# The prompt's mixer input in two tiles, loaded by chunks, and a place of its own for every second mixer weight

## The chip, the cores and the metric

One core of one Trainium2 chip. The time is device microseconds of one execution of the whole program; the number that is compared is the median of several runs. Engines: TensorE (PE: matmuls; its weight loads are called PEld), VectorE (DVE), ScalarE (ACT), GpSimd (POOL) and SyncE (SP, which here only issues transfers). ACT issues transfers as well: all the weight loads stand in its queue.

## The reference

An encoder layer, applied to two groups of tokens with the same weights: the "prompt" (1024 tokens, `s = 0`) and the "sample" (512 tokens, `s = 1`), each with 16 meta tokens put in front. Model width 1024, feed-forward width 2816, all in fp32:

```python
mix = jnp.concatenate([oa, ob], axis=-1)        # the two attention groups' outputs
h   = x + mix @ w_out                            # the "mixer"
n   = rms_norm(h, g_ffn)
gate = conv3(n @ w_ff_gate)                      # depthwise, width 3, over positions
h   = h + (gelu(gate) * (n @ w_ff_up)) @ w_ff_down
y   = rms_norm(h, g_final)
```

Before it come an RMS norm, one projection `w_in`, and two kinds of attention. The change touches only `mix @ w_out` of the prompt.

## The kernel before

Matrices lie transposed: features on the 128 partitions, tokens along the row. A width of 1024 is eight blocks `k` (or `j` on the output side) of 128. Each fp32 product is made of three matmuls in a rounded format (fp32r): the operand is split into `hi` (a cast by ACT, L125) and `lo` (the difference, by DVE or POOL, L126), and `mm3` (L129) adds `hi*hi` (L131), `hi*lo` (L132) and `lo*hi` (L133).

**Weights.** `load_weight` (L144) fetches one block of 128x1024 fp32 (512 KB) into `w_f`, a raw buffer of which there are two (`NRAW`), then writes `w_hi` and `w_lo` into the pool `g.wp`. That pool has three places for each (`NW = 3`), used in turn by all weights of the second half of the program. A cast of `w_hi` can start when the last matmul that read the place's former content is done.

**The mixer of the prompt** (`mixer_out`, L629, with `whole = False`). The 1026 columns are worked in three chunks of 344, 342 and 340. For a chunk: eight casts `xhi<-h` on ACT and eight differences `xlo<-h` on DVE (L666 to L669), then for each of the eight output blocks `j` a weight `w_out[j]`, 24 matmuls into `ps_s`, the sum with the residual (L681) and the sum of squares (L682, `add_square`, ACT and POOL). So each chunk goes through all eight weights once more, 24 weights in all. `h` is one tile, 128 x 8 x 1026; attention's output lies in `oT` in device memory and is loaded into `h` by ten transfers: seven whole blocks of 1025 columns and, for the last block, one for each chunk (L659 to L662).

**What comes before and after.** A generator interleaves the prompt's attention with the sample's mixer and conv-GLU (`merge`, L823). What is left of the sample (the last `w_down` group, L764 to L771, and its final norm, L784 to L797) is drained, and beside it the prompt's mixer begins. Then the prompt's conv-GLU runs to the end of the program; its first step (`normed`, L702) normalises chunks 0 and 1 already beside the mixer's later chunks.

**Order of the work.** On each engine the instructions stand in one fixed order, set when the program is built: a planner lays out all instructions by its own estimates of when each would be free to go, and each engine then takes its list from the top. An instruction that waits holds up all behind it on its engine. PE therefore never picks another matmul when one waits.

Of the kernel before, what the change touches and what calls it, by code (L numbers as in the profile page):

```python
# [13 lines left out]
F32 = mybir.dt.float32  # L14
F32R = mybir.dt.float32r
# [6 lines left out]
P = 128  # L22
# [118 lines left out]
                     xhi[k][:, c0:c0 + cw], xlo[k][:, c0:c0 + cw], i == 0, i == KT - 1)  # L141


def load_weight(g, src, lo_engine=None, hi_engine=None):  # L144

    nc = g.nc
    w = g.wp.tile([P, D], F32, name="w_f", tag="w_f", bufs=NRAW)
    nc.scalar.dma_start(out=w, in_=src)
    hi = g.wp.tile([P, D], F32R, name="w_hi", tag="w_hi")
    lo = g.wp.tile([P, D], F32R, name="w_lo", tag="w_lo")  # L150
    if hi_engine:
        hi_engine.tensor_copy(hi, w)
        nc.vector.tensor_tensor(out=lo, in0=w, in1=hi.bitcast(F32), op=ALU.subtract)
    else:
        split(g, hi, lo, w, lo_engine)
    return hi, lo
# [454 lines left out]
def add_square(g, tp, acc, h, j, c0, cw, eng, bufs=2):  # L611

    nc = g.nc
    hs = h[:, j, c0:c0 + cw]
    if j == 0:
        nc.scalar.activation(acc, hs, AF.Square)
    else:
        sq = tp.tile([P, cw], F32, name="sq", tag="sq", bufs=bufs)
        nc.scalar.activation(sq, hs, AF.Square)
        eng.tensor_tensor(out=acc, in0=acc, in1=sq, op=ALU.add)  # L620
# [8 lines left out]
def mixer_out(g, s, st, side, whole, tag):  # L629

    nc, tc = g.nc, g.tc
    C = SEQS[s] + 2
    h, rstd = st.h, st.rstd
    chunks = token_chunks(s)
    cm = max(w for _, w in chunks)
    with ExitStack() as es:
        mp = pool(es, g, f"fm{s}", 3, side)
        waiting = []

        def finish():  # L640
            while waiting:
                c0, cw, acc = waiting.pop(0)
                mean_rsqrt(g, mp, rstd[:, c0:c0 + cw], acc, cw, tag)

        for group in ([chunks] if whole else [[c] for c in chunks]):
            if whole:
                (xhi, xlo), base = [[x[:, k] for k in range(KT)] for x in st.x], 0
            else:
                xhi = [mp.tile([P, cm], F32R, name="xhi", tag=f"xhi{k}", bufs=2) for k in range(KT)]
                xlo = [mp.tile([P, cm], F32R, name="xlo", tag=f"xlo{k}", bufs=2) for k in range(KT)]  # L650
                base = group[0][0]
            if whole or group[0] != chunks[-1]:
                acc = mp.tile([P, sum(w for _, w in group)], F32, name="acc", tag="acc", bufs=1 if whole else 2)
            else:
                acc = st.tail.tile([P, cm], F32, name="acc_tail")[:, :group[0][1]]
            if group[0][0] == 0:

                nc.vector.memset(h[:, :, C - 1:], 0.0)
                for k in range(KT):  # L659
                    for c0, cw in [(0, C - 1)] if whole or k < KT - 1 else chunks:  # L660
                        cw = min(cw, C - 1 - c0)
                        nc.sync.dma_start(out=h[:, k, c0:c0 + cw], in_=g.oT[s][k * P:(k + 1) * P, c0:c0 + cw])  # L662
            with ExitStack() as behind:
                for mark in g.marks if whole else ():
                    behind.enter_context(tc.issue_after(mark))
                for k in range(KT):  # L666
                    for c0, cw in group:
                        b = c0 - base
                        split(g, xhi[k][:, b:b + cw], xlo[k][:, b:b + cw], h[:, k, c0:c0 + cw])  # L669
            for j in range(KT):  # L670
                w = load_weight(g, g.w_out[j])
                for c0, cw in group:
                    real = min(cw, C - 1 - c0)
                    res = mp.tile([P, cm], F32, name="res", tag="res", bufs=4)[:, :cw]
                    nc.sync.dma_start(out=res[:, :real],
                                      in_=g.xT[s][j * P:(j + 1) * P, NMETA - 1 + c0:NMETA - 1 + c0 + real])
                    if real < cw:
                        nc.vector.memset(res[:, real:], 0.0)
                    ps = g.psum.tile(P, cw, tag)
                    dense(g, ps, w, xhi, xlo, c0 - base, cw)  # L680
                    nc.vector.tensor_tensor(out=h[:, j, c0:c0 + cw], in0=ps, in1=res, op=ALU.add)  # L681
                    add_square(g, mp, acc[:, c0 - base:c0 - base + cw], h, j, c0, cw, nc.gpsimd, 1)  # L682
                    yield 24 * cw
                if j == ML:
                    finish()
            waiting += [(c0, cw, acc[:, c0 - base:c0 - base + cw]) for c0, cw in group]
        if whole:
            finish()
        else:
            st.last = waiting.pop()  # L690


def conv_glu(ctx, g, s, st, side, gb):
# [8 lines left out]
    def normed(np_, c0, cw):  # L702
        for k in range(KT):
            t = np_.tile([P, cw], F32, name="t", tag="t")
            nc.vector.scalar_tensor_tensor(out=t, in0=h[:, k, c0:c0 + cw],
                                           scalar=g.gain[:, V_GFFN + k:V_GFFN + k + 1],
                                           in1=rstd[:, c0:c0 + cw], op0=ALU.mult, op1=ALU.mult)
            split(g, xhi[k][:, c0:c0 + cw], xlo[k][:, c0:c0 + cw], t, nc.gpsimd if s == 1 or k % 2 else nc.vector)
# [13 lines left out]
    for f0 in range(0, NFF, G):  # L722
# [42 lines left out]
        def down(j, c0, cw):  # L765
            ps = g.psum.tile(P, cw, "mm")
            for i, ((ahi, alo), (dhi, dlo)) in enumerate(zip(acts, wd)):
                mm3(g, ps, dhi[:, j * P:(j + 1) * P], dlo[:, j * P:(j + 1) * P],
                    ahi[:, c0:c0 + cw], alo[:, c0:c0 + cw], i == 0, i == len(acts) - 1)
            hs = h[:, j, 1 + c0:1 + c0 + cw]  # L770
            nc.vector.tensor_tensor(out=hs, in0=ps, in1=hs, op=ALU.add)  # L771

        if grp[-1] < NFF - 1:
# [10 lines left out]
        def finish(c0, acc, sums):  # L784
            rs = rstd[:, 1 + c0:1 + c0 + cw]
            if sums:
                rsqrt_newton(g, op, rs, acc, cw)
            else:
                mean_rsqrt(g, op, rs, acc, cw)
            for k in range(KT):  # L790
                y = op.tile([P, ob, cw], F32, name="y", tag="y", bufs=2 if s == 1 else 4) if k % ob == 0 else y
                hs, gk = h[:, k, 1 + c0:1 + c0 + cw], g.gain[:, V_GFIN + k:V_GFIN + k + 1]
                if k % 4 == 3:
                    nc.scalar.activation(y[:, k % ob], hs, AF.Copy, scale=gk)
                    nc.gpsimd.tensor_tensor(out=y[:, k % ob], in0=y[:, k % ob], in1=rs, op=ALU.mult)
                else:
                    nc.vector.scalar_tensor_tensor(out=y[:, k % ob], in0=hs, scalar=gk, in1=rs,  # L797
                                                   op0=ALU.mult, op1=ALU.mult)
                if (k + 1) % ob == 0:
                    nc.sync.dma_start(out=yv[:, k + 1 - ob:k + 1, c0:c0 + cw], in_=y)  # L800

        waiting = None
        for c0 in range(0, N, cw):

            sums = s == 0 and c0 + cw == N
            acc = g.psum.tile(P, cw, "mm") if sums else op.tile([P, cw], F32, name="acc", tag="acc", bufs=ob)
            for j in range(KT):
                down(j, c0, cw)
                if sums:
                    sq = op.tile([P, cw], F32, name="sq", tag="sq_p", bufs=4 * ob)  # L810
                    nc.scalar.activation(sq, h[:, j, 1 + c0:1 + c0 + cw], AF.Square)
                    nc.tensor.matmul(acc, lhsT=g.ones_d, rhs=sq, start=j == 0, stop=j == KT - 1)
                else:
                    add_square(g, op, acc, h, j, 1 + c0, cw, nc.gpsimd if j < PADD else nc.vector, 2)
                if j == LAG and waiting:
                    finish(*waiting)
                yield 3 * len(grp) * cw
            waiting = c0, acc, sums
# [29 lines left out]
LAG = 5  # L848
PADD = 8
ML = 2  # L850
NRAW, NW = 2, 3
R1, R2 = (1.0, 1.1), (1.0, 1.0)
LEAD1, LEAD2, HOLD, STATS = -20000.0, 120000.0, 4, 26

# [2 lines left out]
def trunk_kernel(ctx, tc, g):  # L857
# [61 lines left out]
    def state(es, s, side, with_x):  # L919
        C = SEQS[s] + 2  # L920
        st = Ctx()
        hp = pool(es, g, f"fh{s}", 1, side)
        if with_x:
            st.x = [hp.tile([P, KT, C], F32R, name=nm) for nm in ("xhi", "xlo")]
        st.h = hp.tile([P, KT, C], F32, name="h")
        st.rstd = hp.tile([P, C], F32, name="rstd")
        st.tail = hp
        return st
# [105 lines left out]
```

## Time and profile before

| | |
|---|---|
| median of 3 runs | 2184.26 us (2183.82 to 2185.66) |
| profiled execution, its own time | 2184.81 us |
| span of the profile | 2182.7 us |
| PE busy | 2114.2 us, 97% of the span |
| mean granted TensorE clock | 0.989 |
| prompt's mixer, first matmul to the first `w_gate` matmul | 1309.1 to 1421.3 us |

The time of the profiled execution is 2.1 us more than its span: work ahead of the first and behind the last recorded instruction. In a row of the timeline stand the start, the duration, the engine (ACTq and SPq are the queues that issue transfers), the line, the operation with its tiles, and in square brackets how long the engine had been idle and what ended that. The durations of matmuls are modelled, and each overlaps the next: the pace is read from start to start. In a table of windows, each row gives the window, its length, each engine's busy time with the number of instructions, then the clock that was granted to PE (1.00 is full speed), the share of the transfer engines and the rate in GB/s.

### The profile page before, as it was taken

What the parts mean: (1) busy time and instruction counts of PE and PEld (TensorE: products, weight loads), DVE (VectorE), ACT (ScalarE), POOL (GpSimd) and SP (SyncE); (2) the same over time, 40 slices, a digit from 0 to 9 for tenths busy, and PEclk for the clock granted to TensorE, in tenths of its full rate; (3) what the DMA queues carried; (4) which work ended last, traced back from release to release, by engine and by line L of the source; (5) the groups of instructions that cost most, each with busy time, mean ns of one, the idle gap of its engine ahead of it and who ended that gap; (6) DMA issues with size and microseconds to landing.
All of it is one profiled execution on the core that took longest, in us unless ns stands there. A gap on an engine that the chain in (4) does not pass through costs nothing.

```text
span 2182.7 us, 32285 instructions
## 1 busy us (share of the span) xinstructions
PE 2114.2 (97%) x12442; PEld 1899.7 (87%) x12442; DVE 1319.2 (60%) x2288; ACT 1024.9 (47%) x1803; POOL 624.0 (29%) x465
## 2 busy tenths in 40 slices
PE   8999999988999999999999998999999999999997
PEld 7889999986897888898889898988888888888886
DVE  7645565777767667677777766754434344443346
ACT  6434545667756444677777645542121222112224
POOL 5763444310123222344454314530011100111004
PEclk9999999989999999999999999999999999999999
DMA  6663445563233223232332126511111111111112
GB/s 237 214 218 110 149 156 172 162 209 93 76 94 90 88 68 92 90 108 96 110 111 88 65 88 213 183 68 47 41 49 39 58 49 49 44 34 58 49 39 78
DMA packets 112137, 222.77 MB, mean 102 GB/s; under 512 B 14064, under 2 KB 65520, under 8 KB 111472
## 3 DMA queue, kind: packets, MB, share of 16 engines
q1 hardware_dynamic: 83184, 115.84, 16.7%
q10 hardware_dynamic: 28800, 104.87, 14.7%
q8 instruction: 98, 1.61, 0.3%
q14 instruction: 55, 0.45, 0.1%
HBM read 172.11 MB, written 48.55 MB: 101 GB/s over the span
## 4 chain that ended last, share of the span: by engine, by line
PE 82%; DVE 8%; ACT 3%; issue 3%; DMA 2%; POOL 1%; SPq 0%; ACTq 0%; DVEq 0%; POOLq 0%
PE ps_mm L131 20%; PE ps_mm L132 20%; PE ps_mm L133 20%; PE ps_t L467 5%; PE ps_s L446 4%; PE ps_s L447 3%; PE ps_o L482 2%; DVE p L450 1%; PE ps_o L481 1%; PE ps_o L479 1%; DVE w_lo L126 1%; PE ps_o L477 1%; PE ps_o L478 1%; DVE y L797 1%; DVE pt_lo L126 1%
## 5 line engine op out<-in xcount | busy, mean ns | idle before, releaser
L131 PE MATMUL ps_mm<-xhi,w_hi 128*128 128x512 f32 (+6 forms) x2112 | 703.4, 334 | 2.6 <-DVE hn L117 2.5
L133 PE MATMUL ps_mm<-xhi,w_lo 128*128 128x512 f32 (+6 forms) x2112 | 698.1, 331 | 0.0
L132 PE MATMUL ps_mm<-xlo,w_hi 128*128 128x512 f32 (+6 forms) x2112 | 697.9, 331 | 0.0
L131 PEld LDWEIGHTS ps_mm<-xhi,w_hi 128*128 128x128 f32 x2112 | 400.0, 190 | 28.4 <-DVE hn L117 3.1
L132 PEld LDWEIGHTS ps_mm<-xlo,w_hi 128*128 128x128 f32 x2112 | 399.4, 189 | 25.0 <-issue 0.5
L133 PEld LDWEIGHTS ps_mm<-xhi,w_lo 128*128 128x128 f32 x2112 | 399.2, 189 | 24.4 <-issue 0.5
L125 ACT CAST w_hi<-w_f 128x1024 fp32r<-128x1024 f32 x134 | 139.2, 1047 | 389.9 <-PE ps_mm L132 359.4
L126 POOL TENSOR_TENSOR a_lo<-gate,a_hi 128x512 fp32r<-128x512 f32 x66 | 100.7, 1525 | 651.8 <-ACT a_hi L125 651.6
L450 DVE TENSOR_SCALAR_CACHE_REDUCE p<-ps_s 128x1044 f32<-128x1044 f32 (+7 forms) x212 | 223.3, 1053 | 92.8 <-PE ps_s L447 77.1
L125 ACT CAST pt_hi<-ps_t 128x512 fp32r<-128x512 f32 (+8 forms) x360 | 171.0, 484 | 197.2 <-PE ps_t L467 180.3
L771 DVE TENSOR_TENSOR h<-ps_mm,h 128x512 f32<-128x512 f32 (+1 forms) x288 | 182.3, 645 | 123.7 <-PE ps_mm L133 122.8
L453 ACT ACTIVATE p<-p,nm 128x1040 f32<-128x1040 f32 (+7 forms) x212 | 215.3, 1016 | 85.2 <-DVE p L450 84.4
L126 DVE TENSOR_TENSOR pt_lo<-ps_t,pt_hi 128x512 fp32r<-128x512 f32 (+6 forms) x312 | 173.1, 564 | 102.4 <-ACT pt_hi L125 101.4
L131 PE MATMUL ps_mm<-a_hi,w_hi 128*128 128x512 f32 (+1 forms) x576 | 214.6, 384 | 1.2 <-ACT a_hi L125 1.2
L132 PE MATMUL ps_mm<-a_lo,w_hi 128*128 128x512 f32 (+1 forms) x576 | 215.3, 377 | 0.0
L133 PE MATMUL ps_mm<-a_hi,w_lo 128*128 128x512 f32 (+1 forms) x576 | 215.0, 376 | 0.0
L446 PE MATMUL ps_s<-k,q 128*128 128x348 f32 (+6 forms) x552 | 180.2, 332 | 16.5 <-DVE p L450 16.1
L467 PE MATMUL ps_t<-ident,p 128*128 128x128 f32 (+10 forms) x1188 | 183.8, 269 | 0.3 <-ACT r_rows L502 0.3
L447 PE MATMUL ps_s<-k,q 128*128 128x348 f32 (+6 forms) x552 | 173.7, 320 | 0.0
L126 DVE TENSOR_TENSOR w_lo<-w_f,w_hi 128x1024 fp32r<-128x1024 f32 x100 | 123.4, 1243 | 78.0 <-ACT w_hi L125 77.8
L467 PEld LDWEIGHTS ps_t<-ident,p 128*128 128x128 f32 (+10 forms) x1188 | 142.4, 136 | 29.1 <-issue 4.1
L759 DVE TENSOR_TENSOR gate<-ps_mm,gate 128x512 f32<-128x512 f32 x66 | 45.6, 690 | 186.8 <-PE ps_mm L133 184.6
(200 smaller groups left out, 3367.3 us busy)
## 6 DMA issues: line engine op xcount, KB each, us to landing
w_f<-w_gate ACTq DMA_DIRECT2D x44, 512.0 KB, 3.4
w_f<-w_up ACTq DMA_DIRECT2D x44, 512.0 KB, 3.4
w_f<-w_down ACTq DMA_DIRECT2D x44, 512.0 KB, 4.3
w_f<-w_in ACTq DMA_DIRECT2D x36, 512.0 KB, 3.4
w_f<-w_out ACTq DMA_DIRECT2D x32, 512.0 KB, 3.8
q<-qk SPq DMA_DIRECT2D x48, 257.0 KB, 3.8
qk<-hi SPq DMA_DIRECT2D x20, 384.0 KB, 2.5
qk<-hi SPq DMA_DIRECT2D x20, 272.0 KB, 3.2
```

The lines of the kernel that those rows point to most:

```text
L125: return (nc.scalar.copy(hi, src), (lo_engine or nc.vector).tensor_tensor(out=lo, in0=src, in1=hi.bitcast(F32), op=ALU.subtract))
L126: (lo_engine or nc.vector).tensor_tensor(out=lo, in0=src, in1=hi.bitcast(F32), op=ALU.subtract))
L131: nc.tensor.matmul(ps, lhsT=whi, rhs=xhi, start=start, stop=False)
L132: nc.tensor.matmul(ps, lhsT=whi, rhs=xlo, start=False, stop=False)
L133: return nc.tensor.matmul(ps, lhsT=wlo, rhs=xhi, start=False, stop=stop).ins
L446: nc.tensor.matmul(ps[:, i], lhsT=q[0], rhs=kc, start=True, stop=False)
L447: nc.tensor.matmul(ps[:, i], lhsT=q[1], rhs=kc, start=False, stop=True)
L450: g.evicted = nc.vector.tensor_scalar(out=p.rearrange("p (i w) -> p i w", i=nch), in0=ps, scalar1=-HD ** -0.5, scalar2=3.0e38, op0=ALU.mul ...
L453: nc.scalar.activation(p, p, AF.Exp, bias=nm, scale=-1.0, accum_out=l)
L467: nc.tensor.transpose(tps[:, c:c + M], p[:, k0:k0 + kw], g.ident[:M, :M])
L759: nc.vector.tensor_tensor(out=a, in0=up, in1=a, op=ALU.mult)
L771: nc.vector.tensor_tensor(out=hs, in0=ps, in1=hs, op=ALU.add)
```

## The change

Four things are altered. (1) The prompt's `h` is now two tiles, blocks 0 to 5 and blocks 6 and 7 (`EARLY = 6`); `h[k]` is a list of views of them, and the other edits of `h[:, k, ...]` to `h[k][:, ...]` are only this. The sample's `h` stays one tile. (2) The load goes chunk by chunk: for each of three chunks one transfer of blocks 0 to 5 (128 x 6 x 344 values) and one each for blocks 6 and 7, nine in all. (3) In the prompt's mixer the weights with even `j` take `w_hi` and `w_lo` from the mixer's own pool `mp`, in a place of their own with one buffer (`MW = 1`). (4) The odd ones, and all other weights, keep the three places of `g.wp`.

```diff
@@ -141,13 +141,12 @@
                      xhi[k][:, c0:c0 + cw], xlo[k][:, c0:c0 + cw], i == 0, i == KT - 1)
 
 
-def load_weight(g, src, lo_engine=None, hi_engine=None):
+def load_weight(g, src, lo_engine=None, hi_engine=None, wp=None):
 
     nc = g.nc
     w = g.wp.tile([P, D], F32, name="w_f", tag="w_f", bufs=NRAW)
     nc.scalar.dma_start(out=w, in_=src)
-    hi = g.wp.tile([P, D], F32R, name="w_hi", tag="w_hi")
-    lo = g.wp.tile([P, D], F32R, name="w_lo", tag="w_lo")
+    hi, lo = [(wp or g.wp).tile([P, D], F32R, name=nm, tag=nm, bufs=MW if wp else NW) for nm in ("w_hi", "w_lo")]
     if hi_engine:
         hi_engine.tensor_copy(hi, w)
         nc.vector.tensor_tensor(out=lo, in0=w, in1=hi.bitcast(F32), op=ALU.subtract)
@@ -611,7 +610,7 @@
 def add_square(g, tp, acc, h, j, c0, cw, eng, bufs=2):
 
     nc = g.nc
-    hs = h[:, j, c0:c0 + cw]
+    hs = h[j][:, c0:c0 + cw]
     if j == 0:
         nc.scalar.activation(acc, hs, AF.Square)
     else:
@@ -655,20 +654,27 @@
                 acc = st.tail.tile([P, cm], F32, name="acc_tail")[:, :group[0][1]]
             if group[0][0] == 0:
 
-                nc.vector.memset(h[:, :, C - 1:], 0.0)
-                for k in range(KT):
-                    for c0, cw in [(0, C - 1)] if whole or k < KT - 1 else chunks:
-                        cw = min(cw, C - 1 - c0)
-                        nc.sync.dma_start(out=h[:, k, c0:c0 + cw], in_=g.oT[s][k * P:(k + 1) * P, c0:c0 + cw])
+                for part in st.parts:
+                    nc.vector.memset(part[:, :, C - 1:], 0.0)
+                if whole:
+                    for k in range(KT):
+                        nc.sync.dma_start(out=h[k][:, 0:C - 1], in_=g.oT[s][k * P:(k + 1) * P, 0:C - 1])
+                else:
+                    rows = g.oT[s].rearrange("(k p) t -> p k t", p=P)
+                    for c0, cw in chunks:
+                        cc = slice(c0, min(c0 + cw, C - 1))
+                        nc.sync.dma_start(out=st.parts[0][:, :, cc], in_=rows[:, 0:EARLY, cc])
+                        for k in range(EARLY, KT):
+                            nc.sync.dma_start(out=h[k][:, cc], in_=rows[:, k, cc])
             with ExitStack() as behind:
                 for mark in g.marks if whole else ():
                     behind.enter_context(tc.issue_after(mark))
                 for k in range(KT):
                     for c0, cw in group:
                         b = c0 - base
-                        split(g, xhi[k][:, b:b + cw], xlo[k][:, b:b + cw], h[:, k, c0:c0 + cw])
+                        split(g, xhi[k][:, b:b + cw], xlo[k][:, b:b + cw], h[k][:, c0:c0 + cw])
             for j in range(KT):
-                w = load_weight(g, g.w_out[j])
+                w = load_weight(g, g.w_out[j], wp=None if whole or j % 2 else mp)
                 for c0, cw in group:
                     real = min(cw, C - 1 - c0)
                     res = mp.tile([P, cm], F32, name="res", tag="res", bufs=4)[:, :cw]
@@ -678,7 +684,7 @@
                         nc.vector.memset(res[:, real:], 0.0)
                     ps = g.psum.tile(P, cw, tag)
                     dense(g, ps, w, xhi, xlo, c0 - base, cw)
-                    nc.vector.tensor_tensor(out=h[:, j, c0:c0 + cw], in0=ps, in1=res, op=ALU.add)
+                    nc.vector.tensor_tensor(out=h[j][:, c0:c0 + cw], in0=ps, in1=res, op=ALU.add)
                     add_square(g, mp, acc[:, c0 - base:c0 - base + cw], h, j, c0, cw, nc.gpsimd, 1)
                     yield 24 * cw
                 if j == ML:
...
@@ -848,7 +854,7 @@
 LAG = 5
 PADD = 8
 ML = 2
-NRAW, NW = 2, 3
+NRAW, NW, MW, EARLY = 2, 3, 1, 6
 R1, R2 = (1.0, 1.1), (1.0, 1.0)
 LEAD1, LEAD2, HOLD, STATS = -20000.0, 120000.0, 4, 26
 
@@ -922,7 +928,8 @@
         hp = pool(es, g, f"fh{s}", 1, side)
         if with_x:
             st.x = [hp.tile([P, KT, C], F32R, name=nm) for nm in ("xhi", "xlo")]
-        st.h = hp.tile([P, KT, C], F32, name="h")
+        st.parts = [hp.tile([P, m, C], F32, name=f"h{i}") for i, m in enumerate((KT,) if with_x else (EARLY, KT - EARLY))]
+        st.h = [part[:, k] for part in st.parts for k in range(part.shape[1])]
         st.rstd = hp.tile([P, C], F32, name="rstd")
         st.tail = hp
         return st
```

The planner lays the new program out again, so the lists of the engines change around this stage. Ahead of about 1297 us, and from the prompt's conv-GLU on, the lists are the same but for line numbers and a few places.

**First place, ACT and PE where the mixer begins.** `o_b`, `o_sq`, `rs_y` and `o_rs` belong to the last attention block of the prompt; `acc` and `sq` of 128x256 are the sample's final sum of squares. ACT before, where the first mixer weight is cast, and further down where the mixer's input is cast:

```order
L125 CAST a_hi<-gate 128x512 [waits DVE_49]
L148 DMA w_f<-w_out 128x1024 [waits DMAHW4_49,DMAHW2_49,DVE_49]
L125 CAST w_hi<-w_f 128x1024 [waits DMAHW3_49,PE_49]
L125 CAST pt_hi<-ps_t 128x338 [waits PE_49]
L125 CAST a_hi<-gate 128x512 [waits DVE_49]
```

```order
L587 ACTIVATE o_sq<-o_b 128x338 [waits Activation_49]
L125 CAST xhi<-h 128x344 [waits DMAHW7_49]
L125 CAST xhi<-h 128x342
L114 ACTIVATE rs_y<-ps_t,eps_v 128x338 [waits PE_49]
L125 CAST xhi<-h 128x344 [waits DMAHW0_49]
L125 CAST xhi<-h 128x342
L115 ACTIVATE rs_y<-rs_y 128x338 [waits Activation_49]
```

ACT now, from `o_sq` on:

```order
L586 ACTIVATE o_sq<-o_b 128x338 [waits Activation_49]
L114 ACTIVATE rs_y<-ps_t,eps_v 128x338 [waits PE_49]
L115 ACTIVATE rs_y<-rs_y 128x338 [waits Activation_49]
L116 ACTIVATE o_rs<-rs_y 128x338 [waits Activation_49]
L615 ACTIVATE acc<-h_6015 128x256 [waits DVE_49,Activation_49]
L618 ACTIVATE sq<-h_6015 128x256 x2
L125 CAST xhi<-h_15294 128x344 [waits DMAHW7_49]
L125 CAST xhi<-h_15294 128x344 x5
L125 CAST xhi<-h_15295 128x344 [waits DMAHW0_49]
L125 CAST xhi<-h_15295 128x344 [waits DMAHW1_49]
L125 CAST w_hi<-w_f 128x1024 [waits DMAHW3_49]
```

The early cast of a mixer weight is now that of `w_out[1]` (an odd one, in the shared places); the cast of `w_out[0]` is the last row here. It stands behind the eight casts of the chunk, which stand behind the attention block's norm and the sample's `acc`. On PE the matmuls of the mixer's first chunk stood between those of the sample's last `w_down` pairs (`ps_mm<-a_hi`); now the first of them stands behind all of these and waits for ACT. PE before, and now:

```order
L133 MATMUL ps_mm<-a_hi,w_lo 128x256
L131 MATMUL ps_s<-xhi,w_hi 128x344 [waits Activation_49]
L131 MATMUL ps_mm<-a_hi,w_hi 128x256 [waits DVE_49]
L132 MATMUL ps_mm<-a_lo,w_hi 128x256
L133 MATMUL ps_mm<-a_hi,w_lo 128x256
```

```order
L131 MATMUL ps_mm<-a_hi,w_hi 128x256
L132 MATMUL ps_mm<-a_lo,w_hi 128x256
L133 MATMUL ps_mm<-a_hi,w_lo 128x256
L131 MATMUL ps_s<-xhi,w_hi 128x344 [waits Activation_49]
L132 MATMUL ps_s<-xlo,w_hi 128x344 [waits DVE_49]
```

**Second place, PE and ACT where one even weight follows another.** The numbers tell the tiles apart. PE before, at the change from the second chunk's last weight (15937) to the third chunk's first (16007), and now, where the second chunk's seventh weight (15901) is followed by the third chunk's first (16008) and second (16044):

```order
L132 MATMUL ps_s_15943<-xlo_15652,w_hi_15937 128x342
L133 MATMUL ps_s_15943<-xhi_15644,w_lo_15938 128x342
L131 MATMUL ps_s_16014<-xhi_15972,w_hi_16007 128x340 [waits DVE_49,Activation_49]
L132 MATMUL ps_s_16014<-xlo_15980,w_hi_16007 128x340
L133 MATMUL ps_s_16014<-xhi_15972,w_lo_16008 128x340 [waits DVE_49]
```

```order
L132 MATMUL ps_s_15907<-xlo_15652,w_hi_15901 128x342
L133 MATMUL ps_s_15907<-xhi_15645,w_lo_15902 128x342
L131 MATMUL ps_s_16015<-xhi_15973,w_hi_16008 128x340 [waits Activation_49]
L132 MATMUL ps_s_16015<-xlo_15981,w_hi_16008 128x340
L131 MATMUL ps_s_16051<-xhi_15973,w_hi_16044 128x340 [waits DVE_49]
L132 MATMUL ps_s_16051<-xlo_15981,w_hi_16044 128x340
L133 MATMUL ps_s_16051<-xhi_15973,w_lo_16045 128x340 [waits DVE_49]
```

ACT now, at the same place:

```order
L125 CAST w_hi_15901<-w_f_15899 128x1024 [waits DMAHW2_49,PE_49]
L618 ACTIVATE sq_15859<-h0_15294 128x342 [waits DVE_49,Pool_49]
L148 DMA w_f_16042<-w_out 128x1024 [waits DVE_49]
L618 ACTIVATE sq_15896<-h0_15294 128x342 [waits Pool_49]
L125 CAST w_hi_16044<-w_f_16042 128x1024 [waits DMAHW1_49]
L148 DMA w_f_16080<-w_out 128x1024 [waits DMAHW3_49,DVE_49]
L125 CAST w_hi_16008<-w_f_16006 128x1024 [waits DMAHW7_49,PE_49]
```

Casts of odd weights (16044) no longer wait for PE; those of even weights (15901, 16008) do, and the matmul that PE must have done is the last one that read the even weight before. PE works two matmuls of an even weight, then the 24 of the odd one, then the 22 that are left of the even one, so that between the last matmul that reads the `w_hi` of one even weight (15901) and the first that reads the next one (16008) only one matmul is left here. At the six other changes of this kind from the first chunk's end on there are 6, 3, 1, 1, 4 and 1.

**Third place, SP, the loads of the mixer's input.** Before, and now (the wait `PE_49` of the first load of `h` is for the last transposes of the prompt's attention before, and for a much earlier matmul of it now; the two loads of `h_15295` keep the late wait):

```order
L608 DMA oT_73<-o_b 128x342 [waits DMAHW5_49,DVE_49]
L662 DMA h<-oT_73 128x1025 [waits DMAHW2_49,DMAHW1_49,DMAHW3_49,PE_49,DMAHW7_49,Activation_49,Pool_49]
L662 DMA h<-oT_73 128x1025 [waits DMAHW0_49]
L662 DMA h<-oT_73 128x1025 [waits DMAHW1_49]
L662 DMA h<-oT_73 128x1025 [waits DMAHW2_49]
```

```order
L607 DMA oT_73<-o_b 128x342 [waits DMAHW5_49,DVE_49]
L666 DMA h_15294<-oT_73 128x6x344 [waits DMAHW3_49,DMAHW2_49,DMAHW7_49,DMAHW1_49,PE_49]
L668 DMA h_15295<-oT_73 128x344 [waits PE_49,DMAHW0_49,Activation_49,Pool_49]
L668 DMA h_15295<-oT_73 128x344 [waits DMAHW1_49]
L666 DMA h_15294<-oT_73 128x6x342 [waits DMAHW2_49]
```

The first transfer of blocks 0 to 5 can now be issued right behind the store of the attention block before the last.

More of the change, by code (lines that the diff above doesn't have):

```diff
@@ L704, in normed @@
             t = np_.tile([P, cw], F32, name="t", tag="t")
-            nc.vector.scalar_tensor_tensor(out=t, in0=h[:, k, c0:c0 + cw],
+            nc.vector.scalar_tensor_tensor(out=t, in0=h[k][:, c0:c0 + cw],
                                            scalar=g.gain[:, V_GFFN + k:V_GFFN + k + 1],
@@ L769, in down @@
                     ahi[:, c0:c0 + cw], alo[:, c0:c0 + cw], i == 0, i == len(acts) - 1)
-            hs = h[:, j, 1 + c0:1 + c0 + cw]
+            hs = h[j][:, 1 + c0:1 + c0 + cw]
             nc.vector.tensor_tensor(out=hs, in0=ps, in1=hs, op=ALU.add)
@@ L791, in finish @@
                 y = op.tile([P, ob, cw], F32, name="y", tag="y", bufs=2 if s == 1 else 4) if k % ob == 0 else y
-                hs, gk = h[:, k, 1 + c0:1 + c0 + cw], g.gain[:, V_GFIN + k:V_GFIN + k + 1]
+                hs, gk = h[k][:, 1 + c0:1 + c0 + cw], g.gain[:, V_GFIN + k:V_GFIN + k + 1]
                 if k % 4 == 3:
@@ L810, in conv_glu @@
                     sq = op.tile([P, cw], F32, name="sq", tag="sq_p", bufs=4 * ob)
-                    nc.scalar.activation(sq, h[:, j, 1 + c0:1 + c0 + cw], AF.Square)
+                    nc.scalar.activation(sq, h[j][:, 1 + c0:1 + c0 + cw], AF.Square)
                     nc.tensor.matmul(acc, lhsT=g.ones_d, rhs=sq, start=j == 0, stop=j == KT - 1)
```

## The prediction

> **What bounds the kernel now.** First the page of the profile: the busy shares and the chain of waits.
>
> ```profile
> span 2182.7 us, 32285 instructions
> PE 2114.2 (97%) x12442; PEld 1899.7 (87%) x12442; DVE 1319.2 (60%) x2288; ACT 1024.9 (47%) x1803; POOL 624.0 (29%) x465
> PE 82%; DVE 8%; ACT 3%; issue 3%; DMA 2%; POOL 1%; SPq 0%; ACTq 0%; DVEq 0%; POOLq 0%
> ```
>
> PE sets the time: what an edit is worth is PE time won or lost. Next the table of windows over the stage that is changed, from the last transposes of the prompt's attention to the first gate matmul. Its PE column shows where there is anything to win.
>
> ```profile
> core 0: us, PE busy (x) PEld busy (x) DVE busy (x) ACT busy (x) POOL busy (x), PEclk, DMA share, GB/s
> 1296.00:1308.00 12.00, 12.00 (x93) 11.62 (x92) 7.71 (x17) 5.39 (x11) 1.47 (x1) 1.00 0.53 158
> 1308.00:1321.49 13.49, 10.75 (x65) 8.34 (x63) 12.06 (x28) 9.72 (x23) 0.00 (x0) 1.00 0.83 315
> 1321.49:1328.31 6.82, 6.19 (x22) 6.19 (x23) 0.57 (x1) 3.55 (x9) 5.54 (x7) 0.50 0.43 131
> 1328.31:1343.00 14.69, 12.15 (x64) 10.92 (x64) 9.89 (x13) 8.39 (x16) 10.13 (x10) 0.88 0.50 146
> 1343.00:1421.30 78.30, 77.68 (x489) 76.67 (x489) 60.72 (x91) 43.57 (x74) 36.21 (x27) 1.00 0.59 191
> ```
>
> From 1308 to 1343 PE is idle for 2.74 + 0.63 + 2.54 = 5.9 us, and it loses clock: half of 6.82 us, and 0.12 of 14.69, together 5.2 us. So the handover to the mixer holds about 11 us that could be won at most. The long stage behind it, 78.3 us, has 0.6 us idle: nothing can be won there, only lost.
>
> Third, the timeline in the handover, PE first, then ACT and DVE.
>
> ```profile
> 1309.14 0.32 PE L131 MATMUL ps_s<-xhi,w_hi 128*128 128x344 f32 x1
> 1315.93 0.42 PE L132 MATMUL ps_s<-xlo,w_hi 128*128 128x344 f32 x1 [0.47 <-DVE xlo L126]
> 1317.60 0.42 PE L132 MATMUL ps_s<-xlo,w_hi 128*128 128x344 f32 x1 [0.93 <-DVE xlo L126]
> 1319.30 0.42 PE L132 MATMUL ps_s<-xlo,w_hi 128*128 128x344 f32 x1
> 1320.86 0.42 PE L131 MATMUL ps_s<-xhi,w_hi 128*128 128x344 f32 x1 [0.98 <-ACT w_hi L125]
> 1321.12 0.32 PE L132 MATMUL ps_s<-xlo,w_hi 128*128 128x344 f32 x1
> 1322.12 0.65 PE L133 MATMUL ps_s<-xhi,w_lo 128*128 128x344 f32 x1 [0.68 <-DVE w_lo L126]
> ...
> 1296.68 1.05 ACT L125 CAST w_hi<-w_f 128x1024 fp32r<-128x1024 f32 x1 [3.78 <-PE ps_mm L132]
> 1307.13 0.49 ACT L587 ACTIVATE o_sq<-o_b 128x338 f32<-128x338 f32 x1
> 1308.37 0.86 ACT L125 CAST xhi<-h 128x344 fp32r<-128x344 f32 x2 [0.75 <-DMA h<-oT]
> 1309.14 0.54 ACT L114 ACTIVATE rs_y<-ps_t,eps_v 128x338 f32<-128x338 f32 x1
> 1312.02 0.48 ACT L116 ACTIVATE o_rs<-rs_y 128x338 f32<-128x338 f32 x1
> 1319.76 1.04 ACT L125 CAST w_hi<-w_f 128x1024 fp32r<-128x1024 f32 x1 [1.73 <-PE ps_s L132]
> 1320.71 0.41 ACT L616 ACTIVATE acc<-h 128x256 f32<-128x256 f32 x1
> 1321.03 0.71 ACT L619 ACTIVATE sq<-h 128x256 f32<-128x256 f32 x2
> ...
> 1304.71 4.44 SPq L662 DMA_DIRECT2D h<-oT  x9
> ...
> 1312.96 0.56 DVE L117 SCALAR_TENSOR_TENSOR o_rs<-ps_t,eps_v,o_rs 128x338 f32<-128x338 f32 x1
> 1314.20 0.50 DVE L119 SCALAR_TENSOR_TENSOR o_rs<-o_rs,rs_y 128x338 f32<-128x338 f32 x1
> ```
>
> The input of the mixer is issued at 1304.71, only when attention's transposes are done, and its blocks trickle in between ACT's other work: PE waits for `xlo` at 1315.93 and 1317.60. Then it waits for the second weight. The row at 1319.30 is the last matmul that reads the `w_hi` in whose place the next one goes. The cast starts at 1319.76 and PE goes on at 1320.86. From start to start that is 1.56 us with one matmul between: **this is the price of a weight whose place comes free only when PE has used up the one before**, and the main term below.
>
> **The change part by part.** *The early load.* The first transfer of blocks 0 to 5 is freed from the wait for the last transposes, so its 1.06 MB can land several us before the present 1308. It saves nothing by itself: in the new list of ACT the eight `xhi` casts stand behind the `acc` of the sample, and so does the cast of the first weight. Those I cost now.
>
> *The start of the mixer on PE.* Now its first matmul goes at 1309.14, since its `w_hi` was cast at 1296.68. In the new list the chain is: `o_sq`, the `ps_t` sum on PE, three steps of `rs_y` and `o_rs` on ACT, two on DVE, `acc`, two `sq`, eight casts, the cast of `w_hi`. The early cast of an odd weight (1.05) now stands among attention's casts of `pt_hi` instead, and waits there for a transfer issued at 1295.81, so the chain starts 0 to 1.5 us later than the present 1309.14 at L114. By durations: 0.54 + 0.48 + 0.48 + 0.56 + 0.50 = 2.6 (the second step of ACT taken like the third), `acc` and `sq` 0.41 + 0.71, eight casts at 0.43 (half of 0.86) 3.4, and `w_hi` 1.04: 8.1 us. PE thus starts between 1317.3 and 1320.5 with the hops between engines; I take 1318.5 to 1319.5, ten us later than now. What PE has until then are the sample's six pairs, which it now does among the mixer's; the five pairs left, thirty matmuls of 256 columns, take 3.5 us (an estimate from the pace of 0.158 for 342 columns, read below) and end near 1313. So PE idles about 5.8 us in one piece, where it now idles 2.7 in pieces.
>
> In return the input is complete, and the second weight needs no PE: both waits at 1315.93 and 1317.60 and those at 1320.86 and 1322.12 go, 3.06 us. Laid end to end by the durations of these rows, equal work then comes at about equal time near 1336, and 2 to 5 us earlier near 1345, where two further casts wait less. The handover is worth **-3 us**, between -6 and +3.
>
> *The even weights.* Their one place serves twelve weights, and the next even weight's cast waits until PE's last matmul on the one before. At seven changes from the first chunk's end on, the order leaves 6, 3, 1, 1, 1, 4 and 1 matmuls between that one and the first that needs the new weight. The matmul's pace is read here, four starts in 0.63 us, 0.158 each:
>
> ```profile
> 1371.82 0.32 PE L131 MATMUL ps_s<-xhi,w_hi 128*128 128x342 f32 x1
> ...
> 1372.45 0.32 PE L132 MATMUL ps_s<-xlo,w_hi 128*128 128x342 f32 x1
> ```
>
> A change costs 1.56 us less the pace of what PE does meanwhile, (1 + m) x 0.158, plus 0.10 since the first matmul after a wait takes 0.26 (1320.86 to 1321.12). For m = 1 that is 1.34. Summed over the seven: 10.92 - 24 x 0.158 + 0.70 = **7.8 us**. Nothing covers it: PE stands in order, the waiting matmul is at its head, and behind it stand the 24 of an odd weight which is cast already. Before, this stage had 0.6 us idle, since three places let every cast run a weight ahead.
>
> *What stands ahead of those casts.* 7.8 holds only if ACT and DVE are free when PE is done. The rows that say what may be in the way:
>
> ```profile
> L125 ACT CAST w_hi<-w_f 128x1024 fp32r<-128x1024 f32 x134 | 139.2, 1047 | 389.9 <-PE ps_mm L132 359.4
> L126 DVE TENSOR_TENSOR w_lo<-w_f,w_hi 128x1024 fp32r<-128x1024 f32 x100 | 123.4, 1243 | 78.0 <-ACT w_hi L125 77.8
> w_f<-w_out ACTq DMA_DIRECT2D x32, 512.0 KB, 3.8
> L705 DVE SCALAR_TENSOR_TENSOR t<-h,gain,rstd 128x344 f32<-128x344 f32 x8 | 6.1, 807 | 0.1
> L126 DVE TENSOR_TENSOR xlo<-t,xhi 128x344 fp32r<-128x344 f32 x4 | 3.8, 957 | 0.0
> ```
>
> An odd weight's cast often stands just ahead of the even one's, and waits for its transfer (3.8 us from issue), which ACT issues only behind the eight casts of the next chunk; the even cast is held with it. In the worst two changes I find the even cast 2 us late, once behind such a load and its own 1.05 us, once behind a load that waited for a `w_lo` in DVE's row of `t` and `xlo` (0.81 + 0.96 for a block). Laying the new lists end to end with the durations of these rows (each instruction starts when its engine is free and what it waits for is done) gives 3.3 us at these two, 1.1 to 2.3 at the others, 15.5 in all: **+7.7 us** beyond the floor, between 0 and 9. The same reckoning on the lists of before puts the first gate matmul at 1419.3 to 1420.9, against 1421.3 measured; on the new ones at 1429.7 to 1440.3.
>
> *The clock.* How long an idle piece must be to cost clock is seen in rows of one length:
>
> ```profile
> 1314.66:1318.08 3.42, 2.02 (x13) 1.46 (x11) 3.42 (x10) 2.52 (x7) 0.00 (x0) 1.00 1.04 372
> 1318.08:1321.49 3.41, 2.15 (x9) 1.05 (x7) 2.76 (x6) 1.73 (x4) 0.00 (x0) 1.00 0.25 87
> 1324.90:1328.31 3.41, 3.41 (x14) 3.41 (x14) 0.00 (x0) 1.67 (x4) 2.38 (x4) 0.50 0.05 18
> 1335.14:1338.55 3.41, 1.55 (x7) 0.81 (x6) 2.89 (x5) 3.05 (x6) 2.22 (x3) 1.00 0.36 118
> 1338.55:1341.97 3.42, 3.42 (x13) 3.42 (x13) 2.17 (x2) 0.00 (x0) 2.96 (x3) 0.50 0.86 224
> ...
> 1336.19 0.42 PE L131 MATMUL ps_s<-xhi,w_hi 128*128 128x344 f32 x1 [0.89 <-ACT w_hi L125]
> ```
>
> A window that is 1.55 of 3.41 busy is followed by one at half clock, two of 2.0 to 2.2 by two. The idle 5.8 us must bring one or two such windows, 1.7 us lost in each; before there are three (5.2 us), and that difference is in the handover's term. Of the seven changes only those of 3.3 us can halve the clock: 0 to 3.4, **+1**.
>
> The Trainium skill ("TensorE: Matmul & The Clock Gate", "Why this matters for your kernels") asks for no gap over about 3 us, since one idle window brings half the clock. The window at 1335.14 disagrees: it was 45% busy, the longest idle piece in it 0.89 us, and half clock followed. By the page only the two longest stalls come near, and the sum would be up to 1 us less.
>
> Sum: -3 + 7.8 + 7.7 + 1 = +13.5 on the profiled execution's 2184.81, 2198.3. That execution lies 0.55 above the median of the runs, so against them **2197.8 us**.
>
> **The rivals.** *Floor only.* The even casts find ACT free, and the handover wins a little more: -4 + 7.8, **2188 us**. For it: ACT is busy for only 43.57 of 78.3 us in this stage. Against: it is a queue in order, and the two loads above are issued late by its list.
>
> *Faster.* The early load and the cast of the second weight without PE win back most of the handover's 11 us, and the changes between even weights hide behind PE's queue: **2174 us**. It decides if PE starts the mixer no later than 1309 and each change idles under 0.2 us. For it: DVE's two `xlo` waits and the halved windows are what an early load removes. Against: the cast that the first matmul needs stands behind `acc` in ACT's list, and no order hides 1.56 us behind one matmul.
>
> *More clock lost.* Each longer stall is followed by a half window, four in all, and the handover gains nothing: 15.5 + 3 x 1.7 = 20.6, **2205 us**. For it: 45% busy was enough once. Against: most changes idle 1.1 to 2.3 us, and two windows of 2.0 to 2.2 us busy were needed for that.
>
> *No change.* The planner's list costs in one place what it wins in the other: 2184 us. It would need a handover that wins 15, more than the 11 that are there, or half of it and stalls below the floor.
>
> **How the numbers follow.** Forecast (+8 to +18): 0.62. Floor only: 0.17. More clock: 0.09. Faster: 0.08. No change: 0.04. This kernel's measurement tells about 0.2%, 4.4 us. The forecast, the clock's case and half of the floor's are slower: 0.80. The other half, with no change, lies within: 0.12. Faster 0.08. The range of the forecast's own terms is 2192 to 2204; with the floor's case and the bounds of the clock 2186 to 2206.
>
> **What would show it.** The first `ps_s<-xhi,w_hi` near 1319 behind one idle piece of 5 to 7 us that ends with ACT's `w_hi`, and no wait for `xlo` behind it. Seven or more idle pieces of 1 to 3.3 us between 1345 and 1430, each ending with ACT's `w_hi`, in place of 0.6 us of idle time. The first gate matmul near 1435; from there on the same rows as before. I am wrong if the mixer starts on PE before 1312, or if the stalls of the even weights add up to less than 4 us.

## The result, and the profile after

The changed kernel takes 2200.83 us (median of 4 runs, 2199.99 to 2203.19), the kernel before 2184.04 us beside it. The ratio is 1.0078, with a 95% interval of 1.0065 to 1.0090: 16.8 us slower. 2197.8 us was forecast, with a range of 2186 to 2206. The profiled execution of the changed kernel is the slowest of its four (2203.19 us), so its rows show 2.4 us more than the median has.

From the page of the changed kernel, the span and the busy shares:

```profile
span 2201.4 us, 32262 instructions
PE 2120.0 (96%) x12442; PEld 1905.3 (87%) x12442; DVE 1320.5 (60%) x2289; ACT 1024.3 (47%) x1803; POOL 622.7 (28%) x465
```

The matmuls, ACT, DVE and POOL are what they were. PE works the same number of matmuls, and its busy time has grown by 5.8 us: more of them ran at a lower clock (mean granted clock 0.985 against 0.989). The rest of the span's 18.7 us is idle time. The table of windows says where, with the same columns and the same first five windows as before:

```profile
core 0: us, PE busy (x) PEld busy (x) DVE busy (x) ACT busy (x) POOL busy (x), PEclk, DMA share, GB/s
1296.00:1308.00 12.00, 11.02 (x80) 10.21 (x78) 7.16 (x17) 4.42 (x9) 1.29 (x1) 1.00 0.60 194
1308.00:1321.49 13.49, 8.95 (x60) 8.44 (x59) 10.65 (x24) 9.61 (x25) 1.66 (x2) 0.88 0.81 256
1321.49:1328.31 6.82, 6.82 (x35) 6.75 (x34) 2.86 (x7) 3.25 (x10) 6.19 (x5) 0.74 0.49 157
1328.31:1343.00 14.69, 13.96 (x91) 13.58 (x90) 11.66 (x15) 9.69 (x20) 11.37 (x10) 1.00 0.56 164
1343.00:1421.30 78.30, 65.04 (x368) 62.11 (x367) 49.70 (x75) 34.48 (x59) 25.28 (x21) 0.93 0.52 161
1421.30:1440.00 18.70, 16.67 (x106) 16.12 (x105) 14.58 (x21) 9.99 (x16) 8.49 (x7) 1.00 0.44 147
```

Up to 1343 the changed kernel is a little ahead (266 matmuls recorded from 1296 on, against 244). From 1343 to 1421.3 PE has 368 matmuls where it had 489, and is idle for 13.3 us where it was for 0.6. PE's timeline, the rows with idle time, names each piece:

```profile
1319.40 0.65 PE L131 MATMUL ps_s<-xhi,w_hi 128*128 128x344 f32 x1 [4.54 <-ACT w_hi L125]
1332.67 0.42 PE L133 MATMUL ps_s<-xhi,w_lo 128*128 128x344 f32 x1 [0.73 <-DVE w_lo L126]
1349.80 0.40 PE L131 MATMUL ps_s<-xhi,w_hi 128*128 128x344 f32 x1 [1.40 <-DVE h L687]
1351.24 0.43 PE L133 MATMUL ps_s<-xhi,w_lo 128*128 128x344 f32 x1 [0.89 <-DVE w_lo L126]
1360.41 0.43 PE L131 MATMUL ps_s<-xhi,w_hi 128*128 128x342 f32 x1 [0.44 <-ACT w_hi L125]
1369.44 0.42 PE L131 MATMUL ps_s<-xhi,w_hi 128*128 128x342 f32 x1 [1.16 <-ACT w_hi L125]
1370.78 0.82 PE L624 MATMUL ps_s<-acc,ones_d 128*128 128x344 f32 x2 [0.76 <-DVE h L687]
1381.13 0.43 PE L131 MATMUL ps_s<-xhi,w_hi 128*128 128x342 f32 x1 [2.28 <-ACT w_hi L125]
1391.91 0.43 PE L131 MATMUL ps_s<-xhi,w_hi 128*128 128x342 f32 x1 [2.93 <-ACT w_hi L125]
1402.28 0.42 PE L131 MATMUL ps_s<-xhi,w_hi 128*128 128x340 f32 x1 [0.98 <-ACT w_hi L125]
1412.41 0.43 PE L131 MATMUL ps_s<-xhi,w_hi 128*128 128x340 f32 x1 [2.42 <-ACT w_hi L125]
1422.77 0.43 PE L131 MATMUL ps_s<-xhi,w_hi 128*128 128x340 f32 x1 [0.52 <-ACT w_hi L125]
1431.99 0.43 PE L131 MATMUL ps_s<-xhi,w_hi 128*128 128x340 f32 x1 [1.50 <-ACT w_hi L125]
```

The mixer begins at 1319.40 behind one idle piece. Behind 1360 comes a piece about every 10 us, one for each even weight of the second and third chunk, and each of these eight ends with ACT's `w_hi`. (L687 is DVE's sum of the mixer's output with the residual, L624 the matmuls of the norm's sum of squares.) The first gate matmul starts at 1439.55 where it started at 1421.27; that is 18.3 us, and the span as a whole is 18.7 us longer, so hardly anything is added behind it. PE's waits grouped, from 1345 to 1440 in the changed kernel, with the total, the count and the longest:

```profile
PE ps_s L131 <- ACT w_hi L125: 12.2, 8, 2.9
PE ps_s L131 <- DVE h L687: 1.4, 1, 1.4
PE ps_s L133 <- DVE w_lo L126: 0.9, 1, 0.9
PE ps_s L624 <- DVE h L687: 0.8, 1, 0.8
```

Before, the same view has only 0.6 us, once, for `w_lo`. How the loss is divided is seen by counting matmuls back from the first gate matmul. The last 480 that PE's timeline records start at 1344.19 before and at 1341.19 in the changed kernel. The windows from there to the gate, before and then changed:

```profile
1344.19:1421.27 77.08, 76.46 (x483) 75.51 (x481) 60.69 (x91) 42.96 (x73) 36.18 (x27) 1.00 0.58 189
1341.19:1439.55 98.36, 83.08 (x482) 79.58 (x481) 65.27 (x96) 44.62 (x75) 35.08 (x29) 0.95 0.52 161
```

The same work takes 21.3 us longer, 14.7 of it idle time, the rest a lower clock and slower first matmuls behind each wait.

### The profile page after: what moved, and what is told of

Same layout as the page of the kernel before. It is cut to its first block, busy times and chain, and to the rows that moved or that the text cites. A ratio compares the mean times of both kernels' runs of the same rounds, so it can differ in the third digit from the quotient of the medians.

```text
span 2201.4 us, 32262 instructions
## 1 busy us (share of the span) xinstructions
PE 2120.0 (96%) x12442; PEld 1905.3 (87%) x12442; DVE 1320.5 (60%) x2289; ACT 1024.3 (47%) x1803; POOL 622.7 (28%) x465
## 4 chain that ended last, share of the span: by engine, by line
PE 83%; DVE 8%; ACT 3%; issue 3%; DMA 1%; POOL 1%; ACTq 0%; DVEq 0%; SPq 0%; POOLq 0%
PE ps_mm L131 20%; PE ps_mm L132 20%; PE ps_mm L133 20%; PE ps_t L466 5%; PE ps_s L445 4%; PE ps_s L446 3%; PE ps_o L481 2%; PE ps_o L480 1%; DVE p L449 1%; PE ps_o L478 1%; PE ps_o L476 1%; PE ps_o L477 1%; DVE y L803 1%; DMA w_f<-w_out 1%; DVE w_lo L126 1%
```

## The experiments

The theory: an even weight's single place is wanted again too soon, so PE waits for each cast. The rivals: the load by chunks and the two tiles upset the lists; the mixer's late start on PE is what costs; ACT's queue ahead of the cast costs by itself. The table has all runs. "Start" and "stage" are times in the profiled execution from the last store of `oT` ahead of the mixer's loads (the row `oT<-o_b` of SP, at 1296.29 before and 1296.53 in the changed kernel) to the mixer's first matmul and to the first gate matmul. The executions differ by up to 5.6 us ahead of this stage (the store lies between 1291.0 and 1296.5), so these lengths compare better than the times of the rows. Each ratio is taken against runs of the kernel before that were made beside that kernel (their medians lie between 2183.83 and 2184.83), not against the first row.

| kernel | median us | ratio to before (95%) | start us | stage us |
|---|---|---|---|---|
| before | 2184.04 | 1 | 12.8 | 125.0 |
| changed | 2200.83 | 1.0078 (1.0065 to 1.0090) | 22.9 | 143.0 |
| tiles and chunked load only | 2185.99 | 1.0007 (0.9997 to 1.0016) | 13.6 | 128.7 |
| place for even weights only | 2200.48 | 1.0073 (1.0058 to 1.0088) | 23.6 | 141.2 |
| changed, place for weights 0 and 4 | 2184.52 | 0.9999 (0.9990 to 1.0008) | 22.9 | 124.5 |
| changed, two places for `w_hi` | 2185.68 | 1.0005 (0.9996 to 1.0015) | 22.7 | 126.9 |
| changed, place for odd weights | 2199.93 | 1.0073 (1.0059 to 1.0086) | 16.9 | 142.0 |
| changed, loads on SP | 2199.80 | 1.0072 (1.0056 to 1.0087) | 22.9 | 143.7 |
| changed, place for weights 1 and 5 | 2183.58 | 0.9995 (0.9986 to 1.0004) | 16.9 | 122.2 |
| changed, place for weight 0 | 2180.36 | 0.9983 (0.9974 to 0.9992) | 22.9 | 122.4 |
| before, place for weight 0 | 2179.96 | 0.9979 (0.9969 to 0.9990) | 23.6 | 121.3 |
| changed, place for weight 1 | 2183.81 | 0.9997 (0.9988 to 1.0006) | 16.9 | 124.8 |

### Each half of the change alone

Only the two tiles and the chunked load:

```diff
-                w = load_weight(g, g.w_out[j], wp=None if whole or j % 2 else mp)
+                w = load_weight(g, g.w_out[j])
```

> The two tiles and the chunked load stay, every weight of the mixer goes back to the three shared places. Theory (the even weights' single place costs the time): 2182 to 2187 us, within 0.2% of before; first mixer matmul near 1310, no series of idle pieces ending with w_hi behind 1345. Rival (the load by chunks upsets the lists of ACT and SP): 2193 to 2201 us.

Only the place, put into the kernel before:

```diff
-                w = load_weight(g, g.w_out[j])
+                w = load_weight(g, g.w_out[j], wp=None if whole or j % 2 else mp)
```

> One tile of h and its ten loads as before; only the place of its own for every even weight is added. Theory (single place): 2197 to 2204 us, first mixer matmul near 1319, seven or more idle pieces of 0.4 to 3.3 us ending with ACT's w_hi, as in the changed kernel. Rival (load by chunks): 2182 to 2187 us.

Measured: 2185.99 and 2200.48 us. The first half can't be told from before, the second can't be told from the whole change. PE's waits from 1345 to 1440 in each, the tiles' first:

```profile
PE ps_s L133 <- DVE w_lo L126: 3.2, 5, 1.4
```

```profile
PE ps_s L131 <- ACT w_hi L125: 11.9, 8, 2.2
PE ps_s L133 <- DVE w_lo L126: 0.9, 1, 0.9
...
```

With the place alone there are again eight waits for `w_hi`, of 11.9 us against 12.2, and the late start too (23.6 us). So the place made both, and the rival that blames the load is out. The tiles alone show 3.2 us of waits for `w_lo` in this profile and a stage of 128.7, but their median lies 0.07% above before with an interval that holds 1.

### How soon the place is wanted again

The same place, used by weights 0 and 4 of a chunk only:

```diff
-                w = load_weight(g, g.w_out[j], wp=None if whole or j % 2 else mp)
+                w = load_weight(g, g.w_out[j], wp=None if whole or j % 4 else mp)
```

> As the changed kernel, but only weights 0 and 4 of a chunk use the place of their own, so that 72 matmuls of other weights lie between two users of it. Theory (how soon a place is wanted again): the series of stalls goes, 2180 to 2187 us, although the mixer's first matmul still comes near 1319 to 1321 behind one idle piece of 4 to 6 us. Rival (the late start of the mixer is what costs): 2192 us or more. Rival (clock): half windows behind 1345 remain only if stalls remain.

Measured: 2184.52 us. PE's waits from 1345 to 1440:

```profile
PE ps_s L624 <- DVE h L687: 0.9, 1, 0.9
PE ps_s L131 <- DVE h L687: 0.7, 1, 0.7
PE ps_s L131 <- DVE rstd L117: 0.5, 1, 0.5
```

No wait for `w_hi` is left, and the 16 us are gone. The mixer still starts as late (22.9 us), behind an idle piece of 4.5 us: the late start costs nothing that the median shows. No half window (a stretch of 3.41 us in which PE was granted half its clock) is left behind 1345 either.

Now all even weights again, with two places for `w_hi` and one for `w_lo`; the residual has three buffers instead of four to make room:

```diff
-    hi, lo = [(wp or g.wp).tile([P, D], F32R, name=nm, tag=nm, bufs=MW if wp else NW) for nm in ("w_hi", "w_lo")]
+    hi, lo = [(wp or g.wp).tile([P, D], F32R, name=nm, tag=nm, bufs=n if wp else NW) for nm, n in (("w_hi", 2), ("w_lo", MW))]
```

> As the changed kernel, but the even weights have two places for w_hi (still one for w_lo); to make room the residual has three buffers in the prompt's mixer instead of four. Theory (the cast of w_hi waits for its place): 2181 to 2188 us, idle pieces end with w_lo at most and stay under 1 us each. Rival (ACT's queue, the odd weight's late load ahead of the even cast, costs by itself): the floor of 7.8 us goes and the other 7 to 8 stay, 2191 to 2194 us.

Measured: 2185.68 us, and PE's waits from 1345 to 1440:

```profile
PE ps_s L133 <- DVE w_lo L126: 1.7, 4, 0.5
PE ps_s L131 <- DVE h L687: 1.4, 2, 1.0
PE ps_s L624 <- DVE h L687: 1.2, 1, 1.2
PE ps_s L133 <- DVE res L684: 0.7, 1, 0.7
```

All waits for `w_hi` go, not only the floor of 7.8 us, though ACT's queue has as much in it as before. So here what stands ahead of a cast costs only when the cast must start the moment PE is done. The waits for DVE's sum, up to 1.2 us, were not expected.

### The late start without the stalls, the stalls without the late start

The places swapped, so that the first weight is cast early again:

```diff
-                w = load_weight(g, g.w_out[j], wp=None if whole or j % 2 else mp)
+                w = load_weight(g, g.w_out[j], wp=None if whole or j % 2 == 0 else mp)
```

> As the changed kernel, with the places swapped: odd weights use the single place of their own, even weights the three shared ones. The first weight's cast then goes early again. Theory (the single place costs): 2195 to 2201 us, first mixer matmul near 1312 to 1314 without the idle piece of 4.5 us, and seven or more idle pieces of 0.8 to 4.8 us ending with w_hi behind 1345. Rival (the late start of the mixer costs): 2183 to 2190 us.

Measured: 2199.93 us. The mixer starts 5.9 us earlier than in the changed kernel (16.9 us from the store), with 0.19 us of idle time before it, and the time is as long as the changed kernel's. PE's waits from 1345 to 1440:

```profile
PE ps_s L131 <- ACT w_hi L125: 15.3, 8, 4.3
PE ps_s L133 <- DVE w_lo L126: 1.0, 2, 0.7
```

Together with weights 0 and 4 above (late start, no stalls, no loss) this settles it: the stalls between weights of the single place are the loss.

### What makes a stall longer than its floor

In the changed kernel the stall at 1402.28 is 0.98 us, the value that the kernel before shows at 1320.86 for the same wait. Others reach 2.9 us. ACT's and DVE's rows at the one that ends at 1381.13:

```profile
1377.26 1.05 ACT L125 CAST w_hi<-w_f 128x1024 fp32r<-128x1024 f32 x1 [3.64 <-DMA w_f<-w_out]
1379.60 0.34 ACTq L148 DMA_DIRECT2D w_f<-w_out  x1
1380.03 1.04 ACT L125 CAST w_hi<-w_f 128x1024 fp32r<-128x1024 f32 x1 [0.96 <-DVE w_lo L126]
...
1378.34 1.23 DVE L126 TENSOR_TENSOR w_lo<-w_f,w_hi 128x1024 fp32r<-128x1024 f32 x1 [2.46 <-ACT w_hi L125]
```

The odd weight's cast (1377.26) waits for its load. The next load's issue (1379.60) waits until DVE has made `w_lo` from the raw buffer that it will fill, at 1379.57, and the even weight's cast stands behind that issue. To take the issue out of ACT's queue, the loads of the second and third chunk were moved to SP:

```diff
-    nc.scalar.dma_start(out=w, in_=src)
+    (dma or nc.scalar).dma_start(out=w, in_=src)
...
-                w = load_weight(g, g.w_out[j], wp=None if whole or j % 2 else mp)
+                w = load_weight(g, g.w_out[j], wp=None if whole or j % 2 else mp, dma=nc.sync if group[0][0] else None)
```

> As the changed kernel, but in the second and third chunk the raw weights are loaded from SP's queue instead of ACT's, so that no load that waits for a raw buffer stands ahead of an even weight's cast. If that queue makes the stalls longer than their floor: idle time that ends with w_hi behind 1360 falls from 12.2 to between 7 and 9 us, and the time by 2 to 5 us, if no other wait takes its place. Laid end to end, the lists give about 9 us of it, but 3 us more of waits for the sum on DVE: 2196 to 2201 us.

Measured: 2199.80 us. PE's waits from 1345 to 1440:

```profile
PE ps_s L131 <- ACT w_hi L125: 10.5, 8, 2.5
PE ps_s L131 <- DVE h L687: 4.2, 3, 1.5
PE ps_s L624 <- DVE h L687: 1.3, 1, 1.3
PE ps_s L133 <- DVE w_lo L126: 0.9, 1, 0.9
```

This execution comes 3.5 us earlier, so that its first of the eight stalls starts ahead of 1360, and the expectation's "behind 1360" would count only seven (8.6 us). Over all eight the waits for `w_hi` fall from 12.2 to 10.5, less than was expected. The three longest do fall, from 2.28, 2.93 and 2.42 to 1.49, 0.98 and 1.30, as the queue theory says; but the first and the last grow, from 0.44 and 1.50 to 1.95 and 2.47, and the waits for DVE's sum grow from 2.2 to 5.5. The time does not move. So the load's issue in ACT's list does lengthen the longest stalls, but taking it out of there wins nothing while the single place stays.

### A fourth place that is rarely used

The weights 1 and 5:

```diff
-                w = load_weight(g, g.w_out[j], wp=None if whole or j % 2 else mp)
+                w = load_weight(g, g.w_out[j], wp=None if whole or j % 4 != 1 else mp)
```

> As the changed kernel, but only weights 1 and 5 of a chunk use the place of their own: 72 matmuls lie between its users, and the first weight is cast early. Theory: no series of stalls, first mixer matmul near 1312 to 1314 in place of 1319, gate at 1418 to 1420; 2180 to 2184 us, the best of all so far. Rival (the handover's waits only move): within 2 us of before, 2184 to 2187 us.

Only the first weight of each chunk (`j != 0` in the same condition):

> As the changed kernel, but only the first weight of each chunk uses the place of its own. Theory: no stalls behind 1345 since 168 matmuls lie between its users; the mixer starts late, near 1319, behind one idle piece of 4 to 6 us; gate at 1417 to 1421, 2180 to 2186 us.

The same in the kernel before, with its one tile and ten loads:

> The kernel before (one tile of h, its ten loads) with only the first weight of each chunk in a place of its own. If the two tiles and the chunked load have no part in what the first-weight version won: 2179 to 2182 us, as with them. If they carry it: 2183 to 2185 us, as before.

Only the second weight of each chunk (`j != 1`):

> As the changed kernel, but only the second weight of each chunk (j = 1) uses the place of its own, so that the first weight is cast early into a shared place. If one rarely used fourth place is what wins: 2179 to 2183 us. If the first weight in particular must have it: 2183 to 2186 us.

Measured: 2183.58, 2180.36, 2179.96 and 2183.81 us. The first and the last can't be told from before, and the first one's "best of all" was a miss. A place for the first weight alone is faster than the kernel before, by 0.17% (0.08 to 0.26) with the change's two tiles and chunked load and by 0.21% (0.10 to 0.31) without them; these two have no measurable part in it. PE's waits from 1345 to 1440 in the faster of the two:

```profile
PE ps_s L624 <- POOL y L794: 0.4, 1, 0.4
```

Its mixer begins behind one idle piece of 5.5 us, yet the stage is 3.7 us shorter than before. PE's waits in the whole stage are no shorter (7.3 us of them, against 6.2 before); but one half window is left of three, and the mean granted clock in the stage is 0.99 against 0.96. That would fit a gain by clock, in one profile of each. But the profiles of weight 1 alone and of weights 1 and 5 also show a single half window and a clock of 0.99, and their medians are not faster, so the clock by itself does not explain it. The profiled executions of the two faster kernels are also the fastest of their runs, and 4.8 and 5.3 us of their lead lie ahead of the stage. Why the first weight wins and the second does not stays open.

## Why the prediction was right

*The start of the mixer.* First matmul forecast at 1318.5 to 1319.5, measured 1319.40; the chain was as written, `acc`, two `sq`, eight casts, `w_hi`. The idle piece was 4.54 us instead of 5.8, since the sample's pairs ended at 1314.9 instead of 1313.

*The handover, -3 us.* The stage is 18.0 us longer, the last 480 matmuls of it 21.3 us (98.36 against 77.08). So the part ahead of them is 3.3 us shorter: this term was right.

*The even weights and the queue, 7.8 + 7.7 us.* The seven stalls forecast are the last seven rows of PE's timeline above: 1.16 + 2.28 + 2.93 + 0.98 + 2.42 + 0.52 + 1.50 = 11.8 us idle, 12.5 with the 0.1 of each slow first matmul, where 15.5 stood. The term was sized 3 us too high: two stalls of 3.3 were expected, and the longest was 2.93. Right ahead of the even cast at the long stalls stands the next load's issue, which waits for a raw buffer; at the stall shown the chain begins with the odd weight's late transfer, as the prediction had it. On top came four waits that no term had: for DVE's sum (1.40 and 0.76 us), for a `w_lo` (0.89), and for the `w_hi` of the second chunk's first weight (0.44), less the 0.56 us that was there before.

*The clock, +1 us.* This is the term that was mis-sized most. Three half windows lie behind 1345, 1.7 us lost in each, 5.1 us. Windows of one length with PE's busy time, and what was granted in the next:

```profile
1348.78:1352.20 3.42, 1.51 (x8) 1.26 (x9) 3.39 (x5) 0.90 (x2) 1.88 (x2) 1.00 0.43 129
1352.20:1355.61 3.41, 3.41 (x14) 3.41 (x13) 2.06 (x3) 0.49 (x1) 2.04 (x2) 0.52 0.87 196
1379.50:1382.92 3.42, 1.79 (x11) 1.79 (x12) 3.42 (x7) 2.54 (x5) 1.96 (x3) 1.00 0.59 181
1382.92:1386.33 3.41, 3.41 (x24) 3.41 (x23) 3.41 (x4) 0.63 (x2) 2.75 (x2) 1.00 0.68 215
1389.74:1393.16 3.42, 1.25 (x8) 1.25 (x9) 3.34 (x5) 1.53 (x2) 1.90 (x2) 1.00 0.66 199
1393.16:1396.57 3.41, 3.41 (x14) 3.41 (x14) 0.00 (x0) 0.49 (x2) 1.68 (x2) 0.52 0.62 208
1410.22:1413.64 3.42, 1.23 (x6) 1.03 (x7) 2.34 (x4) 1.47 (x3) 0.81 (x1) 1.00 0.48 154
1413.64:1417.05 3.41, 3.41 (x14) 3.41 (x13) 1.75 (x4) 1.52 (x4) 0.74 (x1) 0.52 0.58 207
...
1368.42:1371.84 3.42, 1.64 (x7) 1.19 (x8) 3.42 (x6) 2.28 (x6) 0.73 (x1) 1.00 0.35 93
1371.84:1375.25 3.41, 3.41 (x24) 3.41 (x23) 1.88 (x4) 1.46 (x4) 1.74 (x2) 1.00 0.94 273
```

The prediction let only stalls of 3.3 us halve the clock. Here the clock was halved behind windows that were 1.51, 1.25 and 1.23 of 3.41 us busy, with idle pieces of 1.40 and 0.89, of 2.93, and of 2.42; it was not behind one of 1.79, with a piece of 2.28, and one of 1.64. In these five rows it goes with the sum of idle time in a window, to which a stall counts only as far as it lies in it. That is no rule yet: of the prediction's two windows of 2.0 to 2.2 us busy, which it read as followed by two half windows, the one of 2.02 is followed by a full one (1318.08, 1.00), the one of 2.15 by a half one. The Trainium skill ("TensorE: Matmul & The Clock Gate", "Why this matters for your kernels") warns of gaps above about 3 us. Behind the mixer's start no gap is that long here (2.93 us at most, and one fall came with pieces of 1.40 and 0.89), and the clock fell three times: the measurement goes against the page's bound.

*The sum.* +13.5 was forecast, against 18.0 in the stage of the profiled executions and 16.8 between the medians: 3.0 too much for the stalls, 4.1 too little for the clock, nothing for waits that came to 2.9, while 0.3 more was won in the handover; 0.8 us of the difference stays unassigned. The mechanism was as forecast; that the number came within 3 us of the median is in part luck, since these errors have both signs. The first gate matmul came at 1439.55, not near 1435, for the same reasons.

*The rivals.* "Floor only" falls with the stalls of 2.3 to 2.9 us. "Faster" falls with the start at 1319.4. "More clock lost" was right on the three half windows of its sum (its text counts four), wrong on a handover that gains nothing; the changed kernel lies between it (2205) and the forecast. "No change" falls with the interval.

## What to carry to other kernels

A buffer that is added does not help if it is tied to a fixed user that wants it back soon: here three shared places plus one reserved for every second weight were slower than three shared ones, while the same place for one weight in four or eight cost nothing or won 0.2%. What matters is how many matmuls the engine's fixed list has between the last reader of a place and the first user of its next content, against the time of the cast that must fit in there. Read that distance from the lists of instructions before the run; one such event in the old trace (1.56 us from start to start here) gives its price.

## What the runs showed of the hardware that was not expected

In the changed kernel the clock was halved for a window of 3.41 us behind windows in which PE was idle in pieces that were each shorter than a window: 1.51 us busy with pieces of 1.40 and 0.89 us was enough, 1.64 and 1.79 us busy were not. Each such window cost 1.7 us, as much as a longer stall itself. In the kernel before, a window of 2.15 us busy was also followed by half clock, so the busy time of these rows alone does not decide it.
